# A two-layer hybrid decoder trunk: the RG-LRU ahead of the SSD's branch, and five smaller moves

## The chip, the cores and the metric

The kernel runs on one core of a Trainium2 chip. Its time is device microseconds (us) of one execution, the median of several runs. Times inside a profile count from the first instruction of the profiled execution.

## The reference, cut to what matters

256 tokens of width 1024 pass two layers, all in float32. `split` stands for the kernel's way of keeping precision: a matrix is taken apart into a high part (fp32r, the format TensorE multiplies in one pass) and the low rest, and a product is three matmuls.

```
c = silu(c);  shift1, scale1, gate1, shift2, scale2, gate2 = split6(c @ ada_w + ada_b)
h = rmsnorm(x) * n1 * (1 + scale1) + shift1
q, k, v, z, xbc, dt, lru_gate, lru_x, merge = split(h @ w_in)           # 16,416 columns
y_attn = three dilated window patterns, 24 heads, softmax over the patterns
y_ssd  = rmsnorm((ssd(silu(conv(xbc)), dt) + D*x) * silu(z), norm_g)    # 2048 wide, 8 groups
a = exp(-8 * sigmoid(x_r) * softplus(-lam))                             # RG-LRU, 1280 wide
y_lru  = scan(a, sqrt(1 - a*a) * sigmoid(x_i) * conv(lru_x)) * gelu(lru_gate)
x = x + gate1 * (sum_b sigmoid(merge_b) * (y_b @ w_br_b)) @ w_out
h = rmsnorm(x) * n2 * (1 + scale2) + shift2
# router: best of 4 groups, then the best 2 of its 8 experts, softmax weights
x = x + gate2 * sum_e weight_e * ((silu(h @ w_gate_e) * (h @ w_up_e)) @ w_down_e)   # 32 experts
out = rmsnorm(x) * final_g
```

## The kernel before

**Pages.** Nearly all data lies in one pool of 42 pages of 512 KB (`Pages`, L131). `Pages.live` counts the pages that are in use as the program is written down. Weights come as loads of one page each through the queue of SyncE (SP), in a fixed order (`Ring`, L148): `pump` writes down the next load while fewer than `ahead` loads stand ready and fewer than 42 - `reserve` pages are live; `take` hands the next one over, and writes its load down on the spot when none is ready. The pairs (ahead, reserve) of the stages stand at L23.

**Dense part.** A layer's products are jobs of 4 to 15 loads (`Job`, L1433). `go_on` (L629) walks the list of (job, load) steps. A step prepares the load four steps ahead (`LEAD`): ScalarE copies the high part `wh`, VectorE and GpSimd take turns at the low part `wl`; the SSD's branch weights are scaled by the norm's weight at the same time (L1449). Then it issues the matmuls of its own load (a step of a merge chunk or branch has 12 with 512 columns), finishes the job before if that is due, and lets at most three side threads run on to their next `yield` (`Side.tick`, L190); a `yield n` puts the thread off for n steps. Side threads are the attention pairs, SSD groups, z gates and the LRU. The planner that places instructions keeps, engine by engine, near to the order written. `act(...)` (L275) chains those ScalarE operations that need a function table.

The order of jobs in a layer is that of `_chunks` (L31): B, C, X and z twice (with the sums for the adaptive norms between), v, q and k; the SSD's merge chunks with its branch (16 loads); `lx`, `lxg`, `lg` for the LRU with the jobs of gate 1, the LRU's own gates (5 loads); the merge chunks and branches of attention and LRU; `w_out`. The LRU thread (`lru`, L1010) starts at the last gate product.

**Experts.** `out_half` (L1084) adds the two halves of the result to x and starts squares and logits. `moe` (L1203) makes the normalised x as `xnh`, has two jobs for the sums of gate 2 (`filler`), chooses experts (`route`), makes the low part `xnl`, and gathers the tokens of four experts as `xe` (`gather`). Then 16 steps of two experts follow: `up_part`, `combine` of the step before, `turn`, `down_part`. An expert has room for 64 tokens; a conditional block (`overflow`, L1361) recomputes the rest if any expert has more. It stands at step 15 and takes its pages from the pool.

Of the kernel before, what the change touches and what calls it, by code (L numbers as in the profile page):

```python
# [30 lines left out]
def _chunks():  # L31
# [20 lines left out]
    for n in range(2):  # L52
        put("m", (n, 1), MG0 + 1024 + 512 * n)
# [5 lines left out]
    for b in (0, 2):  # L59
        for n in range(2):  # L60
            put("m", (n, b), MG0 + 1024 * b + 512 * n)
# [157 lines left out]
class Trunk:  # L219
# [90 lines left out]
    def run(self):  # L310
# [26 lines left out]
        self.filler = {}  # L337
        jobs = self.jobs = [self.layer_jobs(l) for l in range(DEPTH)]
        loads = []
        for l in range(DEPTH):  # L340
            for phase in jobs[l]:
                loads += [j.loads[q] for j, q in phase if q is not None]
            for j in self.filler[l]:
                loads += j.loads
            loads += self.expert_loads(l)
# [60 lines left out]
    def ada_finish(self, job):  # L406
# [4 lines left out]
        if kind == "g":  # L411
            self.copy(co, job.banks[0])
            if i == 0:
                self.gate_page(l, 0)
            g = self.gate[l, i // 2]
            o = g[:, (i % 2) * 512:(i % 2) * 512 + 512]
            self.mm(p, bc(self.const("sel"), [128, 128]), co, True, i < 2)
            if i < 2:
                self.tt(o, p, o, OP.add)
            else:  # L420
                self.spread(p, o[0:1], False)
                self.copy(o, p)
# [101 lines left out]
    def logits(self, n):  # L524
# [3 lines left out]
        for kp in (2 * n, 2 * n + 1):  # L528
            p = self.x_T(kp, self.x)
            o = self.hT[kp // 2][:, 2 * (kp % 2):2 * (kp % 2) + 2]  # L530
# [8 lines left out]
    def layer_jobs(self, l):  # L539
# [89 lines left out]
    def go_on(self):  # L629
        pend = None  # L630
        for i, (j, q) in enumerate(self.seq):
# [5 lines left out]
            if j.kind == "out":  # L637
                self.ring.ahead, self.ring.reserve = OUT
                if q == 0:
                    self.gate_page(self.l, 1)  # L640
                    self.xnh = [self.pages.get([128, 1024], F32R, "xnh") for b in range(2)]
                    self.hT = [self.pages.get([128, 4, 256], F32, "hT") for b in range(2)]
# [73 lines left out]
    def chunk_done(self, job):  # L716
# [24 lines left out]
        elif kind in ("lx", "lxg", "lg"):  # L741
            for t in range(4):
# [7 lines left out]
                else:  # L750
# [3 lines left out]
                    self.copy(self.lg[ti // 4][:, ti % 4], src)  # L754
# [32 lines left out]
    def attn_pair(self, l, hp):  # L787
# [47 lines left out]
        yield 2  # L835
# [37 lines left out]
    def ssd_group(self, l, g):  # L873
# [49 lines left out]
        pz = self.ps().rearrange("p (j t) -> p j t", j=4)  # L923
        for j in range(2):
# [15 lines left out]
    def gate_z(self, l, i, z):  # L940
# [8 lines left out]
        self.split_act(hi, lo, y)  # L949
# [9 lines left out]
        if i == 3:  # L959
            self.yT[1] = self.zT  # L960
            yield 2
# [48 lines left out]
    def lru(self, l):  # L1010
# [3 lines left out]
        for u in range(3):  # L1014
# [3 lines left out]
            sq = self.third(u, "lsq")  # L1018
            self.act(sq, rp[u], AF.Square)
            self.stt(tp[u], sq, 1.0, tp[u], OP.add, OP.mult)  # L1020
            if u < 2:
                self.pages.free()
            yield 2
        for u in range(3):
            self.act(tp[u], tp[u], AF.Sqrt)
            self.tt(ip[u], ip[u], tp[u], OP.mult)
        yield 1
        for u in range(3):
            self.act(self.lg[u], self.lg[u], AF.Gelu_apprx_tanh)
        his, los = [], []  # L1030
        for u in range(3):
            hi, lo = self.third(u, "ylh", F32R), self.third(u, "yll", F32R)
            for t in range(sizes[u]):
                self.nc.vector.tensor_tensor_scan(tp[u][:, t], rp[u][:, t], ip[u][:, t], 0.0, OP.mult, OP.add)  # L1034
            self.tt(tp[u], tp[u], self.lg[u], OP.mult)
            self.split_act(hi, lo, tp[u])
# [4 lines left out]
            yield 2  # L1041
# [8 lines left out]
    def branch_done(self, job):  # L1050
# [14 lines left out]
        if n == 1:  # L1065
            self.pages.free(2 * min(len(self.yT[b][0]), 2 if b == 2 else 4))
# [136 lines left out]
    def moe(self, l):  # L1203
# [7 lines left out]
        for j in self.filler[l]:  # L1211
# [6 lines left out]
        pages.live -= 2  # L1218
        self.xnl = [pages.get([128, 1024], F32R, "xnl") for b in range(2)]
        for b in range(2):  # L1220
            self.stt(self.xnl[b], self.x[b], r[b], self.xnh[b].bitcast(F32), OP.mult, OP.subtract)
# [5 lines left out]
        def gather(j):  # L1227
# [6 lines left out]
            xe = [pages.get([128, 4, 256], F32, "xe") for h in range(2)]  # L1234
# [13 lines left out]
            Sf = S.bitcast(F32)  # L1248
# [14 lines left out]
            st[j] = (xe, ST, ws)  # L1263

        def up_part(i):
# [13 lines left out]
            if i % 2:  # L1279
                pages.free(2)  # L1280
# [50 lines left out]
        ye = None  # L1331
# [286 lines left out]
```

## Time and profile before

| | us |
|---|---|
| median of 3 runs (2285.91 to 2288.2) | 2286.91 |
| the profiled execution | 2287.82 |
| its span, first to last instruction | 2286.1 |
| PE busy in it | 2155.9 (94%) |
| VectorE (DVE) / ScalarE (ACT) / GpSimd (POOL) busy | 1125.2 / 802.5 / 440.8 |
| moved by DMA | 638.76 MB |

A busy PE is not PE at its peak: a matmul's record covers its way through the array, and they overlap. How many start in a stretch says more. Experts run in the stretches where DMA stands at 409 GB/s.

### The profile page before, as it was taken

The page shows a single profiled execution, that of the slowest core. Times are in us where ns is not written, and L with a number is a line of the kernel's source. Part 1 is how long each engine was busy: PE and PEld are TensorE (multiplying, and loading weights), DVE is VectorE, ACT ScalarE, POOL GpSimd, SP SyncE. Part 2 cuts the span into 40 slices and gives each one's busy share as a digit, 9 for nine tenths or more (in the row PEclk, how much of TensorE's full clock was granted, in tenths as well). Part 3 has the DMA queues.
Part 4 walks back from the last instruction along what each step waited for, and adds up shares of the span by engine and source line. Part 5 has one row for each costly group of instructions (what it writes and reads, how often), then busy time and mean ns, then how long its engine had stood idle before and what let it go on. Part 6 is the DMA issues. An engine that isn't in the chain of part 4 may idle for free.

```text
span 2286.1 us, 31957 instructions
## 1 busy us (share of the span) xinstructions
PE 2155.9 (94%) x12432; PEld 1428.4 (62%) x12432; DVE 1125.2 (49%) x1782; ACT 802.5 (35%) x1240; POOL 440.8 (19%) x189
## 2 busy tenths in 40 slices
PE   6999999999899999999989999999989999999997
PEld 4878798787674444333368988878868544443332
DVE  3877767653842222222258876774484322222222
ACT  3555644536531111101145655453474211111111
POOL 2333432232420000000023444212334000000000
PEclk9999999999999999999999999999999899999999
DMA  9565334574588999999994534447557799999996
GB/s 384 172 223 202 125 119 145 196 254 148 202 343 326 409 409 409 409 409 409 369 374 157 166 112 130 122 148 257 177 182 271 286 408 409 409 409 409 409 409 270
DMA packets 178524, 638.76 MB, mean 279 GB/s; under 512 B 20256, under 2 KB 20512, under 8 KB 178368
## 3 DMA queue, kind: packets, MB, share of 16 engines
q1 hardware_dynamic: 176976, 633.55, 74.2%
q8 instruction: 101, 1.65, 0.3%
q0 software_dynamic: 672, 1.74, 0.2%
q10 hardware_dynamic: 720, 1.37, 0.2%
q14 instruction: 55, 0.45, 0.1%
HBM read 635.53 MB, written 1.05 MB: 278 GB/s over the span
## 4 chain that ended last, share of the span: by engine, by line
PE 36%; DMA 7%; DVE 3%; ACT 2%; issue 2%; POOL 0%; DVEq 0%; SPq 0%; ACTq 0%; POOLq 0%
PE pm L265 29%; PE pside L265 6%; DMA w<-in_exp_u_dram 3%; DMA w<-in_exp_g_dram 3%; PE pside L273 1%; DMA w<-in_exp_d_dram 1%; ACT eaT L284 0%; DVE wl L1459 0%; ACT wh L284 0%; DVE Pb L296 0%; ACT Pb L281 0%; DVE lt L1034 0%; DVE mx L299 0%; ACT Pa L281 0%; DVE xbcX L287 0%
## 5 line engine op out<-in xcount | busy, mean ns | idle before, releaser
L1459 POOL TENSOR_TENSOR wl<-w,wh 128x1024 fp32r<-128x1024 f32 (+1 forms) x159 | 411.1, 2593 | 1234.2 <-ACT wh L284 669.9
L265 PE MATMUL pm<-w,xe 128*64 128x512 f32 x2048 | 502.8, 599 | 15.5 <-DMA w<-in_exp_u_dram 8.2
L265 PEld LDWEIGHTS pm<-w,xe 128*64 128x64 f32 x2048 | 166.3, 137 | 321.6 <-issue 238.3
L284 ACT ACTIVATE wh<-w 128x1024 fp32r<-128x1024 f32 (+1 forms) x316 | 306.2, 1012 | 44.0 <-DVE wl L1459 11.6
L265 PE MATMUL pm<-hh,wl 128*128 128x256 f32 x1056 | 303.0, 288 | 6.3 <-DVE wl L1459 4.4
L265 PE MATMUL pm<-hh,wh 128*128 128x256 f32 x1056 | 303.6, 288 | 4.9 <-ACT wh L284 3.1
L1459 DVE TENSOR_TENSOR wl<-w,wh 128x1024 fp32r<-128x1024 f32 (+1 forms) x157 | 267.0, 1704 | 68.3 <-ACT wh L284 65.0
L265 PE MATMUL pm<-hl,wh 128*128 128x256 f32 x1056 | 300.1, 284 | 0.0
L265 PE MATMUL pm<-w,eaT 128*64 128x512 f32 x1024 | 243.2, 597 | 22.2 <-ACT eaT L284 22.2
L287 DVE TENSOR_TENSOR ea<-ea,pm 128x512 f32<-128x512 f32 x32 | 22.0, 688 | 403.5 <-PE pm L265 403.5
L265 PEld LDWEIGHTS pm<-hh,wh 128*128 128x128 f32 x1056 | 203.4, 193 | 20.0 <-ACT wh L284 9.9
L265 PE MATMUL pm<-wh,hh 128*128 128x512 f32 (+1 forms) x544 | 205.6, 378 | 10.1 <-ACT sg L281 10.1
L265 PEld LDWEIGHTS pm<-hh,wl 128*128 128x128 f32 x1056 | 203.2, 193 | 11.5 <-DVE wl L1459 5.1
L265 PEld LDWEIGHTS pm<-hl,wh 128*128 128x128 f32 x1056 | 203.5, 193 | 1.0 <-issue 0.7
L265 PE MATMUL pm<-wh,hl 128*128 128x512 f32 (+1 forms) x544 | 201.8, 371 | 0.0
L265 PE MATMUL pm<-wl,hh 128*128 128x512 f32 (+1 forms) x544 | 201.8, 371 | 0.0
L265 PEld LDWEIGHTS pm<-w,eaT 128*64 128x64 f32 x1024 | 73.9, 137 | 159.4 <-issue 121.0
L281 ACT ACTIVATE ea<-pm 128x512 f32<-128x512 f32 x32 | 19.1, 597 | 298.2 <-PE pm L265 298.2
L265 PEld LDWEIGHTS pm<-wh,hh 128*128 128x128 f32 x544 | 104.1, 191 | 29.4 <-ACT sg L281 12.1
L284 ACT ACTIVATE eaT<-pside 128x512 f32<-128x512 f32 x32 | 19.1, 597 | 290.1 <-PE pside L273 290.1
L265 PEld LDWEIGHTS pm<-wl,hh 128*128 128x128 f32 x544 | 104.1, 191 | 12.8 <-issue 1.6
L265 PEld LDWEIGHTS pm<-wh,hl 128*128 128x128 f32 x544 | 103.7, 191 | 12.6 <-issue 0.7
(308 smaller groups left out, 2974.1 us busy)
## 6 DMA issues: line engine op xcount, KB each, us to landing
w<-in_exp_g_dram SPq DMA_DIRECT2D x256, 512.0 KB, 10.2
w<-in_exp_u_dram SPq DMA_DIRECT2D x256, 512.0 KB, 10.2
w<-in_exp_d_dram SPq DMA_DIRECT2D x256, 512.0 KB, 10.2
w<-in_w_in_dram SPq DMA_DIRECT2D x208, 512.0 KB, 4.1
w<-in_ada_w_dram SPq DMA_DIRECT2D x96, 512.0 KB, 5.0
w<-in_w_br_dram SPq DMA_DIRECT2D x60, 512.0 KB, 4.2
w<-in_w_in_dram SPq DMA_DIRECT2D x64, 384.0 KB, 3.1
w<-in_w_out_dram SPq DMA_DIRECT2D x16, 512.0 KB, 3.7
```

What stands on the lines that cost most here:

```text
L265: return self.nc.tensor.matmul(o, l, r, start=start, stop=stop, skip_group_check=True)
L273: self.nc.tensor.transpose(o, i, self.ident)
L281: self.table_op = self.nc.scalar.activation(out=o, in_=i, func=f, **kw).ins
L284: self.nc.scalar.activation(out=o, in_=i, func=AF.Copy)
L287: self.nc.vector.tensor_tensor(out=o, in0=x, in1=y, op=op)
L1459: eng.tensor_tensor(out=lo, in0=w, in1=hi.bitcast(F32), op=OP.subtract)
```

## The change

- The SSD's merge chunks and branch move behind the LRU's gate products. The LRU thread yields after nearly every operation or pair of scans.
- `gelu` is applied when the gate is copied from PSUM. The three parts of `lsq`, `ylh`, `yll` all use whole pages.
- The norm's weight is put on y (`hi`, `lo` by columns), no longer on the SSD's branch weights.
- The two jobs for gate 2 are ordinary jobs among the chunks of each layer; the bias of gate 2 is fetched broadcast, as that of gate 1.
- `xnl` is made right behind `xnh`, ahead of `route`; `xT` is no longer in `hT` pages.
- `ST` and `ws` of a group of experts are made after the first products (`ways_back`), `xe` and `ye` are held from the start.
- `overflow` stands at step 8 and counts its six pages; the reserves of the expert part change.
- In an SSD group the decay `E` is computed one stage later, in a bank that is in use anyway.

```diff
-N_PAGES, N_HALF = 42, 10
-DENSE, BRANCH, OUT, MOE, MOE_END = (4, 8), (99, 9), (99, 3), (99, 4), (99, 18)
+N_PAGES, N_HALF = 42, 11
+DENSE, BRANCH, OUT, MOE = (4, 8), (99, 9), (99, 4), (99, 0)
+IF_AT, MOE_IF, MOE_CLAIM, MOE_LAST = 8, 6, 7, 3
@@ _chunks
-    for n in range(2):
-        put("m", (n, 1), MG0 + 1024 + 512 * n)
     put("lx", 0, LX0)
...
-    for b in (0, 2):
+    for b in (1, 0, 2):
         for n in range(2):
             put("m", (n, b), MG0 + 1024 * b + 512 * n)
@@ gate_page
-        if i == 0:
-            self.nc.gpsimd.dma_start(g, bass.AP(tensor=src.tensor, offset=src.offset, ap=[[0, 128], [1, 1024]]))
-        else:
-            self.nc.gpsimd.dma_start(g[0:1], src)
+        self.nc.gpsimd.dma_start(g, bass.AP(tensor=src.tensor, offset=src.offset, ap=[[0, 128], [1, 1024]]))
@@ layer_jobs
+        extra += [self.ada_job(l, n, "g", i) for i, n in ((2, 10), (3, 11))]
-        self.filler[l] = [self.ada_job(l, n, "g", i) for i, n in ((2, 10), (3, 11))]
@@ chunk_done, "lg"
-                    self.copy(self.lg[ti // 4][:, ti % 4], src)
+                    self.act(self.lg[ti // 4][:, ti % 4], src, AF.Gelu_apprx_tanh)
@@ gate_z
-        self.split_act(hi, lo, y)
+        for t in range(4):
+            c = self.col(l, "sn")[:, 4 * i + t:4 * i + t + 1]
+            self.act(hi[:, t], y[:, t], AF.Copy, scale=c)
+            self.stt(lo[:, t], y[:, t], c, hi[:, t].bitcast(F32), OP.mult, OP.subtract)
@@ lru
         for u in range(3):
             self.act(tp[u], tp[u], AF.Sqrt)
+        yield 1
+        for u in range(3):
             self.tt(ip[u], ip[u], tp[u], OP.mult)
         yield 1
-        for u in range(3):
-            self.act(self.lg[u], self.lg[u], AF.Gelu_apprx_tanh)
...
-            hi, lo = self.third(u, "ylh", F32R), self.third(u, "yll", F32R)
             for t in range(sizes[u]):
                 self.nc.vector.tensor_tensor_scan(tp[u][:, t], rp[u][:, t], ip[u][:, t], 0.0, OP.mult, OP.add)
+                if t % 2:
+                    yield 1
             self.tt(tp[u], tp[u], self.lg[u], OP.mult)
-            self.split_act(hi, lo, tp[u])
+            yield 1
+            hi, lo = [self.pages.get([128, 4, 256], F32R, n)[:, 0:sizes[u]] for n in ("ylh", "yll")]
+            self.copy(hi, tp[u])
+            yield 1
+            self.tt(lo, tp[u], hi.bitcast(F32), OP.subtract)
...
-            yield 2
+            yield 1
@@ moe
             self.act(self.xnh[b], self.x[b], AF.Copy, True, scale=r[b])
+            self.stt(self.xnl[b], self.x[b], r[b], self.xnh[b].bitcast(F32), OP.mult, OP.subtract)
         self.warm(AF.Exp, r[1])
-        for j in self.filler[l]:
-            for q in range(4):
-                j.prepare(q)
-                j.product(q)
-            j.finish()
         rest = self.route(l, r)
...
+        xe = [pages.get([128, 4, 256], F32, "xe") for h in range(2)]
+        ye = [pages.get([128, 1024], F32R, n) for n in ("yeh", "yel")]
         gather(0)
...
         for i in range(16):
-            if i == 13:
-                ring.ahead, ring.reserve = MOE_END
-            if i == 15:
+            if i == IF_AT - 1:
+                ring.reserve = MOE_IF
+            if i == IF_AT:
                 self.table_op = None
                 self.overflow(l)
                 self.table_op = None
+                ring.reserve = MOE[1]
+            if i == 13:
+                ring.reserve = MOE_CLAIM
...
-            if i % 2 and i + 1 < 16:
+            if i % 2 == 0:
+                ways_back(i // 2)
+            elif i + 1 < 16:
                 gather(i // 2 + 1)
...
+            if i == 14:
+                ring.reserve = MOE_LAST
@@ Job.prepare
-        if self.kind == "branch" and self.arg[2] == 1:
-            s = T.col(self.arg[0], "sn")
-            for k in range(2):
-                c = s[:, 2 * q + k:2 * q + k + 1]
-                T.act(hi[:, k], w[:, k], AF.Copy, scale=c)
-                T.stt(lo[:, k], w[:, k], c, hi[:, k].bitcast(F32), OP.mult, OP.subtract)
-        else:
-            T.copy(hi, w)
...
+        T.copy(hi, w)
...
```

## Rows read from the trace of the kernel before

**Rows 1.** The page's slices: 40 equal parts of the span, DMA in GB/s.

```profile
GB/s 384 172 223 202 125 119 145 196 254 148 202 343 326 409 409 409 409 409 409 369 374 157 166 112 130 122 148 257 177 182 271 286 408 409 409 409 409 409 409 270
```

**Rows 2.** Windows, layer 1: length, busy (instructions) by engine, PEclk, DMA share, GB/s.

```profile
1650.00:1675.00 25.00, 25.00 (x126) 17.91 (x125) 12.52 (x13) 22.72 (x45) 6.95 (x4) 1.00 0.45 148
1675.00:1700.00 25.00, 20.89 (x83) 15.94 (x81) 24.96 (x26) 16.34 (x19) 8.07 (x3) 0.93 0.63 210
```

**Rows 3.** Timeline of PE: start, us, what, [idle before <-who ended it].

```profile
549.14 0.50 PE L265 MATMUL pm<-wh,hh 128*128 128x512 f32 x1
...
593.13 0.79 PE L265 MATMUL pm<-wh,hh 128*128 128x512 f32 x1 [4.32 <-ACT sg L281]
...
1660.72 0.50 PE L265 MATMUL pm<-wh,hh 128*128 128x512 f32 x1
...
1704.71 0.79 PE L265 MATMUL pm<-wh,hh 128*128 128x512 f32 x1 [5.05 <-ACT sg L281]
```

**Rows 4.** Chain of waits in order of time: start, us, what.

```profile
1704.71 29.57 PE pm L265 x120
...
1735.15 24.61 PE pm L265 x108
```

**Rows 5.** DVE groups, 1640 to 1712: count, busy us, mean ns, idle.

```profile
L1459 DVE TENSOR_TENSOR wl<-w,wh 128x1024 fp32r<-128x1024 f32 x9 | 12.4, 1374 | 3.1 <-ACT wh L284 3.1
...
L1034 DVE TENSOR_TENSOR_SCAN lt<-lr,li 128x256 f32<-128x256 f32 x10 | 6.1, 663 | 0.0
```

**Rows 6.** Timeline of PE, one gate job: its four loads, then its sum.

```profile
1590.70 1.92 PE L265 MATMUL pm<-w,c 128*32 128x512 f32 x16
...
1595.79 1.02 PE L265 MATMUL pside<-cond,cn 128*128 128x512 f32 x2
```

**Rows 7.** Waits on DVE: engine, line, <-whom: us in total, times, longest.

```profile
DVE gate L287 <- DMA gate<-in_ada_b_dram: 8.7, 2, 4.5
```

**Rows 8.** Timeline around the router: layer 0's low part first, then layer 1.

```profile
687.20 2.48 DVE L296 SCALAR_TENSOR_TENSOR xnl<-x,rs,xnh 128x1024 fp32r<-128x1024 f32 x2
...
1781.45 0.69 DVE L287 TENSOR_TENSOR ot<-pside,gate 128x512 f32<-128x512 f32 x1 [2.70 <-PE pside L265]
...
1788.89 0.35 DVE L296 SCALAR_TENSOR_TENSOR rgl<-pm,rs,rbias 128x4 f32<-128x4 f32 x2 [2.06 <-PE pm L265]
...
1793.68 0.23 DVE L287 TENSOR_TENSOR rA<-route,roh 128x64 fp32r<-128x64 f32 x1
...
1794.92 2.17 ACT L281 ACTIVATE xnh<-x,rs 128x1024 fp32r<-128x1024 f32 x2
...
1801.03 2.48 DVE L296 SCALAR_TENSOR_TENSOR xnl<-x,rs,xnh 128x1024 fp32r<-128x1024 f32 x2
...
1802.36 0.58 PE L265 MATMUL pside<-S,xnl 128*128 128x256 f32 x1 [2.65 <-DVE xnl L296]
...
1809.33 13.95 PE L265 MATMUL pm<-w,xe 128*64 128x512 f32 x64
```

**Rows 9.** Timeline of SP's expert loads: the last group of eight, and two after.

```profile
1782.60 5.17 SPq L170 DMA_DIRECT2D w<-in_exp_g_dram  x8
...
1799.46 0.33 SPq L170 DMA_DIRECT2D w<-in_exp_u_dram  x1
...
1811.27 0.80 SPq L170 DMA_DIRECT2D w<-in_exp_u_dram  x2
```

**Rows 10.** Windows around the conditional block (layer 0) and the gather (layer 1).

```profile
1120.00:1138.00 18.00, 15.18 (x68) 5.15 (x66) 2.79 (x4) 1.99 (x4) 0.00 (x0) 1.00 0.73 282
...
1800.00:1812.00 12.00, 9.64 (x62) 7.82 (x64) 6.24 (x14) 3.04 (x6) 0.00 (x0) 0.67 0.17 45
```

**Rows 11.** Instructions of tile wl, low parts: ns min/median/max, first and last start.

```profile
L1459 POOL TENSOR_TENSOR wl<-w,wh x159: 1833/2422/3409, 32.6 to 1767.1; 128x1024 fp32r<-128x1024 f32 x127, 128x768 fp32r<-128x768 f32 x32
L1459 DVE TENSOR_TENSOR wl<-w,wh x157: 940/1226/3427, 28.6 to 1764.2; 128x1024 fp32r<-128x1024 f32 x125, 128x768 fp32r<-128x768 f32 x32
```

**Rows 12.** The page's DMA issues: engine, count, size, us from issue to landing.

```profile
w<-in_w_br_dram SPq DMA_DIRECT2D x60, 512.0 KB, 4.2
```

More of the change, by code (lines that the diff above doesn't have):

```diff
@@ L529, in logits @@
             p = self.x_T(kp, self.x)
-            o = self.hT[kp // 2][:, 2 * (kp % 2):2 * (kp % 2) + 2]
+            o = self.half([128, 2, 256], "xT")
             self.copy(o[:, 0], p[:, 0])
@@ L639, in go_on @@
                 if q == 0:
-                    self.gate_page(self.l, 1)
-                    self.xnh = [self.pages.get([128, 1024], F32R, "xnh") for b in range(2)]
-                    self.hT = [self.pages.get([128, 4, 256], F32, "hT") for b in range(2)]
+                    self.xnh, self.xnl = [[self.pages.get([128, 1024], F32R, n) for b in range(2)] for n in ("xnh", "xnl")]
             self.prepare_to(i + (OUT_LEAD if j.kind == "out" else LEAD) + 1)
@@ L923, in ssd_group @@
         pz = self.ps().rearrange("p (j t) -> p j t", j=4)
+        for j in range(2):
+            for e in range(2):
+                h = 4 * g + 2 * j + e
+                self.mm(pz[64 * e:64 * e + 64, 2 + j], bc(self.av[:, 1, h:h + 1], [128, 64]), self.const("le"))
+        self.act(E, pz[:, 2:4], AF.Exp)
         for j in range(2):
@@ L960, in gate_z @@
             self.yT[1] = self.zT
-            yield 2
+            yield 5
             rz = self.k([128, 2], "rz", 2)
@@ L1065, in branch_done @@
         if n == 1:
-            self.pages.free(2 * min(len(self.yT[b][0]), 2 if b == 2 else 4))
+            self.pages.free(2 * len(self.yT[b][0]))
         if b == 2:
@@ L1209, in moe @@
             self.act(self.xnh[b], self.x[b], AF.Copy, True, scale=r[b])
+            self.stt(self.xnl[b], self.x[b], r[b], self.xnh[b].bitcast(F32), OP.mult, OP.subtract)
         self.warm(AF.Exp, r[1])
-        for j in self.filler[l]:
-            for q in range(4):
-                j.prepare(q)
-                j.product(q)
-            j.finish()
         rest = self.route(l, r)
[L1218 to L1221, printed above, removed]
         acol = self.acol[l]
@@ L1294, in down_part @@
         def down_part(i, aT, last=False):
-            yh = pages.get([128, 1024], F32R, "yeh")
-            yl = pages.get([128, 1024], F32R, "yel")
+            yh, yl = ye
             ws = st[i // 2][2][:, i % 2:i % 2 + 1]
@@ L1341, in moe @@
                 self.warm(AF.Sqrt, av[:, 0:1])
-            if ye is not None:
+            if i:
                 for n in range(2):
-                    combine(i - 1, ye, n)
+                    combine(i - 1, n)
             aT = turn(av)
-            if i % 2 and i + 1 < 16:
+            if i % 2 == 0:
+                ways_back(i // 2)
+            elif i + 1 < 16:
                 gather(i // 2 + 1)
@@ L1358, in moe @@
                 self.on_pool = False
-        pages.free(5)
+        pages.free(9)
     def overflow(self, l):
@@ L1366, in overflow @@
             hT = self.hT = [self.pages.get([128, 4, 256], F32, "hT") for h in range(2)]
+            ow = [self.pages.get([128, 2, 512], F32, "ow") for q in range(4)]
             for kp in range(4):
@@ L1380, in overflow @@
                     for q in range(4):
-                        t = self.pages.pool.tile([128, 2, 512], F32, name="ow", tag="page")
+                        t = ow[q]
                         nc.sync.dma_start(t, a[w][l, bass.ds(e, 1), q].rearrange("o p k n -> (o p) k n"))
@@ L1400, in overflow @@
                     for q in range(2):
-                        t = self.pages.pool.tile([128, 2, 512], F32, name="ow", tag="page")
+                        t = ow[2 * n + q]
                         nc.sync.dma_start(t, a["exp_d"][l, bass.ds(e, 1), 2 * n + q].rearrange("o p k n -> (o p) k n"))
@@ L1411, in overflow @@
                         self.stt(self.x[b][:, sl], t, self.wo[:, b, bass.ds(e, 1)], self.x[b][:, sl], OP.mult, OP.add)
-            self.pages.free(2)
+            self.pages.free(6)
     def final_gain(self):
```

51 lines of the change are left out of this document (16 added, 35 removed).

## The prediction

> **What bounds the kernel now.** I read the page's slices first, then tables of windows, the PE rows around its gaps, and SP's issues. The slices show two regimes, twice [rows 1]: in a layer's dense part DMA moves 112 to 286 GB/s in most slices; while the experts run it stands at 409, slice after slice. So the dense part is paid in PE time, the expert part in bytes. An expert load is 512 KB, at 409 GB/s 1.28 us, and there are 384 in a layer. The expert stretch thus ends a fixed time after its first products release pages: anything that makes those products start earlier moves the end by as much.
>
> The dense part has one large hole per layer. In layer 1 PE has 83 matmuls in 25 us, while DVE is busy 24.96 of 25 [rows 2]. The PE rows say where [rows 3]: from the first product of merge chunk (0, 0) to that of (0, 2) there are 144 matmuls, and 43.99 us pass, in both layers (549.14 to 593.13, 1660.72 to 1704.71). At the undisturbed pace of the chain of waits, 24.61 us for 108 matmuls or 0.228 each, they need 32.8 [rows 4]. The last wait is 5.05 us for ACT's sigmoid `sg`, and behind it the chain has 29.57 us for 120 matmuls that would need 27.3. In the code, `sg` stands behind the LRU's copies on ACT, and these wait for DVE's scans and products.
>
> **The change part by part.** *LRU ahead of the SSD's branch.* Behind the last gate product there are then 24 steps of merge and SSD branch, 24 x 12 x 0.228 = 65.7 us, and 36 before the first product that needs the LRU. Its thread takes 22 ticks, one per step. DVE's share in it is four operations over 2560 columns, 3.1 us each by the 1.23 of a 1024-column low part [rows 11], and ten scans at 0.66: 19 us; the low parts of 12 weights at 1.37 are another 16 [rows 5]. That is 35 of 65.7. The hole of 43.99 - 32.8 = 11.2, and 2.2 of the slow run behind it, goes: I take 13 us in each layer. Bounds: 6 (half stays) to 13.4. What is late next is the weights' preparation, below.
>
> *Norm weight on y, gelu at evacuation, E one stage later, `xT` in a half page.* Work moves, little is added. The SSD weights' two scaled copies and two subtractions become one of each, half of them on POOL; four column-wise steps per z chunk replace one. Gelu takes the place of a copy; each extra table change costs ACT 1.28 us beside a PE that is fed four steps ahead. I put nothing; without that cover, 0 to 2 us a layer.
>
> *Gate sums early.* Two jobs of four loads leave the router's stretch and go among the SSD's chunks. PE pays 1.92 for the loads' products and 1.02 for the sum over partitions [rows 6], twice: 5.9 us a layer. The bias page is now fetched whole, as gate 0's is, and DVE stood 8.7 us in two such waits [rows 7]; behind the waiting sum stand convolutions and low parts. PE's share of 4.35 is between 0 and all; nearest is the old wait, in which PE's chunk went on, so I take 1.5. Together 7.4 a layer. POOL's one issue a layer delays its next low part, which is needed four steps on.
>
> *Router.* In layer 1 the last half of x is begun at 1781.45; the logits reach DVE at 1788.89, the choice is done at 1793.91, but PE is then in the second gate job, and `xnl` runs only at 1801.03, since ACT made `xnh` at 1794.92, behind the jobs' copies [rows 8]. PE gathers from 1802.36, the first expert product starts at 1809.33. Without the jobs the logits come some 1.4 earlier (two stretches of 1.06 stood between them), at 1787.5; the choice costs DVE 5.0, the two `xnl` 2.5 beside it: 1795.0. Rank product, positions and S take some 1.6, partly beside `xnl`, so the gather starts near 1796.0. It took 5.96 for 28 of its 32 products, so 6.8, and 0.6 for the last evacuation: 1803.4, a gain of 6 (4 to 8). Layer 0 had the same with a gather that sped up: `xnl` at 687.20; I take 4 (2 to 6). The ways back move behind the first products, worth 1.2 of it.
>
> PE stands idle longer before this gather than now; its granted clock was 0.67 in 1800 to 1812 [rows 10], a mixture of 1.2 and 2.4 GHz, and I counted the gather at the lower pace. The Trainium skill (TensorE: Matmul & The Clock Gate, Part 1: The HAM clock gate) says that an idle array falls to half rate and must be busy again before it is let up. By that rule the whole gather runs low, as I have it; had I counted it at 2.4 GHz the gain would be 9 and the total 6 lower.
>
> *Pages.* At the first expert product 33 loads had been issued: four groups of eight, and one at 1799.46; the next came at 1811.27, when PE freed pages [rows 9]. Counted from the code, `xe` and `ye` are now held from the start: 42 - 11 = 31. The DMA queue is idle then, so two more loads are to be moved after it: 2.6 us a layer (0 to 2.6). The filler's eight loads no longer precede the experts, but the 31 land in time either way.
>
> *The If in the middle.* SP drains its loads there now, too: 282 GB/s over 18 us against 409 is a loss of 5.6 [rows 10]. In a stretch bound by bytes it costs the same at step 8. I put 0 (-5 to +3 a layer). Larger reserves and shares at the end change nothing while DMA stays at 409.
>
> Sum: -26 + 14.8 - 10 + 5.2 = -16. The profiled execution took 2287.82 (span 2286.1 and 1.7 around it), so 2271.8; the median of the runs is 0.9 lower: **2271**, its own range 2263 to 2279.
>
> **The rivals.** *The weights come late (slower).* In the SSD's branch 26 pages are now held (yz 8, LRU 8, the rest 10), four pairs are 8, and the pump stops at 34: twelve to sixteen loads a layer are issued only when they are taken, four steps = 10.9 us ahead of use, where eight steps were usual. Landing takes 4.2 [rows 12], ACT's copy 1.09 as half of `xnh` [rows 8], POOL's part 2.42, at most 3.41 [rows 11]: 7.7 to 8.7, so PE would not notice. But in each queue LRU work stands ahead; with 14 us on the way a step takes 14/4 = 3.5 instead of 2.73, and 32 loads cost 25: 2296. It decides from 12.7 us on, where 32 x 0.45 eats most of the 16. For it: ACT was busy 22.72 of 25 in the gates' stretch [rows 2]. Against: ACT and DVE have more room behind it.
>
> *The hole only shrinks.* DVE blocked by POOL, or ACT by a copy that waits, now inside the SSD's branch: half of 26 stays, 2284. DVE's low part took 1.23 at the median and up to 3.43 [rows 11], and POOL gets twelve more a layer. The Trainium skill (SBUF — State Buffer, Summary: rules for kernel authors) states that where DVE reads two inputs and GpSimd reads too, the second to issue waits out the first; the trace agrees, with 3.43 against 1.23. By it 12 x 2.2 = 26 us join DVE's 35, nearly what the stretch has; it would come out at this rival's time.
>
> *More is gained.* PE has small gaps of its own among the SSD's chunks; the sums vanish in them (-14.8 at most), or the pages' term doesn't show: 2257.
>
> *The If holds SP.* Before, SP waited for its own loads alone. If at step 8 it must wait for pages that PE frees, 25 loads ahead less 8 in flight is up to 17 x 1.15 = 20 us, say 15 a layer: 2301. Nothing in the trace shows such a wait.
>
> **How the numbers follow.** A measurement tells 0.2%, 4.6 us, from no change: faster is below 2282.3, slower above 2291.5. The forecast has 0.55, more gained 0.15, the shrunken hole 0.14 (0.05 of it below 2282.3), late weights 0.11, the held SP 0.05 (0.02 of these two within 0.2%). Faster 0.55 + 0.15 + 0.05 = 0.75, same 0.09 + 0.02 = 0.11, slower 0.14. The range runs from 2254, below the gain without the sums, to 2289, the hole's upper side and the bound of the DVE waits: it leaves out 0.04 below and 0.14 above.
>
> **What would show it.** Right: the windows of the merge and branch chunks all have some 110 matmuls in 25 us; no PE wait for `sg` over 1 us; from `ot` to the first expert product some 22 instead of 28 us in layer 1; 31 loads issued by then; 282 GB/s or so around step 8 and 409 up to the last load. Wrong: PE waits for `wh` or `wl` in the SSD's branch (late weights); DVE at 25 of 25 there (the hole moved); PE gaps in the SSD's chunks behind `gate`; a DMA gap over 10 us at the If.

## The result: 38 us slower, and where they are in the profile after

The changed kernel takes 2325.62 us (median of 4 runs, 2325.17 to 2327.94) against 2287.33 beside it: a ratio of 1.017, 95% interval 1.0152 to 1.0188. The prediction was 2271, with 2254 to 2289 as its range. The profiled execution took 2325.38, its span 2323.6.

Five marks in either trace end the five stages of a layer: DVE's first `rot` (q and k chunks begin), ACT's last `kT`, DVE's first `ot` (the result of `w_out`), PE's first expert product, and DVE's last `x<-x,pside`.

| stage, us in layer 0 / layer 1 | before | after | difference |
|---|---|---|---|
| start to the first q/k chunk | 298.8 / 247.1 | 316.1 / 263.6 | +17.3 / +16.5 |
| q/k chunks | 98.3 / 98.7 | 97.6 / 98.1 | -0.7 / -0.6 |
| last q/k chunk to `w_out` (LRU, branches) | 263.7 / 264.3 | 271.9 / 271.8 | +8.2 / +7.5 |
| router and gather | 33.7 / 36.4 | 28.0 / 28.0 | -5.7 / -8.4 |
| experts | 468.4 / 468.5 | 468.4 / 471.2 | 0.0 / +2.7 |

They sum to 36.8 of the 37.5 us between the spans. Two stages lost, and of these the LRU's was forecast as the main gain.

The page's slices have the same two regimes as before [rows 1]; the expert slices stay at 409:

```profile
GB/s 382 172 209 209 159 138 148 171 111 174 262 326 290 409 409 409 378 409 409 409 360 176 181 135 124 114 138 185 124 256 237 282 409 409 409 378 410 409 409 284
```

The hole moved with the LRU. Windows of layer 1 (columns as in [rows 2]), now beside the SSD's branch:

```profile
1632.00:1657.00 25.00, 24.01 (x111) 16.57 (x111) 12.07 (x12) 23.45 (x44) 8.61 (x4) 1.00 0.34 108
1657.00:1682.00 25.00, 18.38 (x69) 14.35 (x68) 24.59 (x19) 14.64 (x16) 12.20 (x5) 0.87 0.48 166
1682.00:1707.00 25.00, 25.00 (x110) 20.64 (x110) 14.32 (x14) 13.71 (x15) 10.73 (x4) 0.99 0.54 189
```

PE runs 69 matmuls where the windows beside have 110, and DVE is busy for 24.59 of 25. PE's timeline names the wait, which answers to the 5.05 us of [rows 3]:

```profile
1676.51 0.80 PE L265 MATMUL pm<-wl,yzh 128*128 128x512 f32 x1 [5.65 <-DVE wl L1442]
1677.10 0.63 PE L265 MATMUL pm<-wh,yzl 128*128 128x512 f32 x1
1677.53 0.63 PE L265 MATMUL pm<-wh,yzh 128*128 128x512 f32 x1
```

The wait is for a low part of DVE, and matmuls behind it start 0.43 us apart instead of 0.228 [rows 4]: the hole is paid a second time at the low clock. DVE's timeline, and under it GpSimd's, show what the low part stood behind:

```profile
1661.73 1.23 DVE L287 TENSOR_TENSOR li<-li,lt 128x1024 f32<-128x1024 f32 x1 [0.37 <-ACT lt L281]
1662.99 3.94 DVE L1022 TENSOR_TENSOR_SCAN lt<-lr,li 128x256 f32<-128x256 f32 x3
1666.86 6.17 DVE L287 TENSOR_TENSOR li<-li,lt 128x1024 f32<-128x1024 f32 x2
...
1675.25 1.21 DVE L1442 TENSOR_TENSOR wl<-w,wh 128x1024 fp32r<-128x1024 f32 x1
```

```profile
1662.72 2.50 POOL L1442 TENSOR_TENSOR wl<-w,wh 128x1024 fp32r<-128x1024 f32 x1 [4.19 <-ACT wh L284]
1666.77 2.41 POOL L1442 TENSOR_TENSOR wl<-w,wh 128x1024 fp32r<-128x1024 f32 x1 [1.54 <-ACT wh L284]
1669.46 3.01 POOL L1442 TENSOR_TENSOR wl<-w,wh 128x1024 fp32r<-128x1024 f32 x1 [0.29 <-ACT wh L284]
```

A DVE operation with both inputs in SBUF that starts here while GpSimd makes a low part ends only half a us to 1.1 us behind GpSimd's end: the first of the three scans ran from 1662.99 to 1665.77, GpSimd's subtraction from 1662.72 to 1665.22. So two `li` products took 6.17 us, and the three scans 3.94 (0.66 each undisturbed [rows 5]).

In the first stage PE stops behind the second gate job. PE, then DVE, then ACT:

```profile
1316.42 0.39 PE L265 MATMUL pm<-hh,wl 128*128 128x256 f32 x1 [3.96 <-DVE wl L1442]
```

```profile
1309.14 0.69 DVE L287 TENSOR_TENSOR gate<-pside,gate 128x512 f32<-128x512 f32 x1 [1.09 <-PE pside L265]
1309.75 3.32 DVE L296 SCALAR_TENSOR_TENSOR yzl<-xbcX,cols,yzh 128x256 fp32r<-128x256 f32 x4
1313.00 6.70 DVE L1442 TENSOR_TENSOR wl<-w,wh 128x1024 fp32r<-128x1024 f32 x2
```

```profile
1308.07 1.06 ACT L278 ACTIVATE z<-xbcX 128x1024 f32<-128x1024 f32 x1 [3.10 <-DVE cb L881]
1309.03 1.69 ACT L278 ACTIVATE yzh<-xbcX,cols 128x256 fp32r<-128x256 f32 x4
1310.63 6.72 ACT L284 ACTIVATE wh<-w 128x1024 fp32r<-128x1024 f32 x7
```

ACT waits for DVE, the gate sum and the four column-wise copies and subtractions of a z chunk come first, and then seven high parts are due at once. GpSimd's rows of the same time show that DVE is held here, too:

```profile
1309.27 2.73 POOL L944 TENSOR_TENSOR zsum<-zsum,z 128x512 f32<-128x512 f32 x2 [4.98 <-ACT z L278]
1312.70 5.92 POOL L1442 TENSOR_TENSOR wl<-w,wh 128x1024 fp32r<-128x1024 f32 x2 [0.70 <-DVE yzl L296]
```

Of the four subtractions the first two took 1.10 and 1.51 us, beside `zsum`, and the last two 0.47 each; the low part that PE waits for ran from 1313.00 to 1316.37 beside GpSimd's from 1312.70 to 1315.28.

The router, which answers to [rows 8]:

```profile
1824.01 0.69 DVE L287 TENSOR_TENSOR ot<-pside,gate 128x512 f32<-128x512 f32 x1 [2.64 <-PE pside L265]
...
1834.36 0.22 DVE L287 TENSOR_TENSOR rA<-route,roh 128x64 fp32r<-128x64 f32 x1
...
1836.54 2.47 DVE L296 SCALAR_TENSOR_TENSOR xnl<-x,rs,xnh 128x1024 fp32r<-128x1024 f32 x2
```

```profile
1836.37 1.19 PE L265 MATMUL pside<-S,xnh 128*128 128x256 f32 x4 [0.71 <-DVE S L287]
...
1843.54 0.65 PE L265 MATMUL pm<-w,xe 128*64 128x512 f32 x2
```

From `ot` of the last half to the first expert product 19.5 us pass instead of 27.9; `xnl` still runs behind the choice. The windows around the conditional block (layer 0, then 1) answer to [rows 10]:

```profile
940.00:960.00 20.00, 17.43 (x74) 6.56 (x71) 1.92 (x4) 1.23 (x2) 0.00 (x0) 0.91 0.81 314
...
2075.00:2095.00 20.00, 20.00 (x103) 9.01 (x101) 3.75 (x7) 1.19 (x2) 0.00 (x0) 0.92 0.82 322
```

At 409 GB/s as the rate, 314 over 20 us is a loss of 4.6 us and 322 one of 4.3, about 1 us less than the 5.6 counted at step 15.

### The profile page after: what moved, and what is told of

It is laid out like the page before. It is cut to its first block, busy times and chain, and to the rows that moved or that the text cites. A ratio compares the mean times of both kernels' runs of the same rounds, so it can differ in the third digit from the quotient of the medians.

```text
span 2323.6 us, 31904 instructions
## 1 busy us (share of the span) xinstructions
PE 2177.8 (94%) x12424; PEld 1434.8 (62%) x12424; DVE 1128.3 (49%) x1762; ACT 804.3 (35%) x1226; POOL 475.8 (20%) x205
## 3 DMA queue, kind: packets, MB, share of 16 engines
q0 software_dynamic: 896, 2.78, 0.4%
## 5 line engine op out<-in xcount | busy, mean ns | idle before, releaser
L1442 POOL TENSOR_TENSOR wl<-w,wh 128x1024 fp32r<-128x1024 f32 (+1 forms) x175 | 450.7, 2582 | 1246.0 <-ACT wh L284 1125.0
L265 PE MATMUL pm<-w,xe 128*64 128x512 f32 x2048 | 494.5, 600 | 7.6 <-DVEq L1354 5.2
L284 ACT ACTIVATE wh<-w 128x1024 fp32r<-128x1024 f32 (+1 forms) x348 | 342.0, 1017 | 103.1 <-PE pm L265 32.0
L1442 DVE TENSOR_TENSOR wl<-w,wh 128x1024 fp32r<-128x1024 f32 (+1 forms) x173 | 296.2, 1720 | 128.4 <-ACT wh L284 120.9
L265 PEld LDWEIGHTS pm<-w,xe 128*64 128x64 f32 x2048 | 158.8, 137 | 306.9 <-issue 266.5
L265 PE MATMUL pm<-hh,wh 128*128 128x256 f32 x1056 | 309.3, 293 | 5.8 <-ACT wh L284 4.1
L265 PE MATMUL pm<-wh,hh 128*128 128x512 f32 (+1 forms) x544 | 199.6, 371 | 0.0
L284 ACT ACTIVATE yeh<-yt 128x512 fp32r<-128x512 f32 x64 | 40.3, 630 | 248.1 <-DVE yt L296 247.2
L287 DVE TENSOR_TENSOR x<-x,pside 128x512 f32<-128x512 f32 x128 | 83.4, 683 | 81.4 <-PE pside L265 80.5
L296 DVE SCALAR_TENSOR_TENSOR yt<-pm,ws,gate 128x512 f32<-128x512 f32 x64 | 48.1, 751 | 147.1 <-PE pm L265 147.1
## 6 DMA issues: line engine op xcount, KB each, us to landing
w<-in_exp_g_dram SPq DMA_DIRECT2D x256, 512.0 KB, 10.2
w<-in_exp_u_dram SPq DMA_DIRECT2D x256, 512.0 KB, 10.2
w<-in_exp_d_dram SPq DMA_DIRECT2D x256, 512.0 KB, 10.2
```

The lines of the kernel that those rows point to most:

```text
L265: return self.nc.tensor.matmul(o, l, r, start=start, stop=stop, skip_group_check=True)
L284: self.nc.scalar.activation(out=o, in_=i, func=AF.Copy)
L287: self.nc.vector.tensor_tensor(out=o, in0=x, in1=y, op=op)
L296: self.nc.vector.scalar_tensor_tensor(out=o, in0=x, scalar=s, in1=y, op0=op0, op1=op1)
L1442: eng.tensor_tensor(out=lo, in0=w, in1=hi.bitcast(F32), op=OP.subtract)
```

## The experiments

All medians and ratios to the kernel before, which ran beside each (2286.07 to 2288.56); stages as above, layer 0 / 1.

| run | median | ratio (95%) | start to q/k | to `w_out` | router | experts |
|---|---|---|---|---|---|---|
| e1 gates back | 2315.46 | 1.0123 (1.0106-1.0140) | 305.2 / 256.2 | 270.4 / 270.4 | 32.9 / 33.2 | 469.3 / 471.8 |
| e2 SSD first | 2311.96 | 1.0107 (1.0091-1.0124) | 315.2 / 263.4 | 266.3 / 266.3 | 28.0 / 27.0 | 467.9 / 471.4 |
| e3 both back | 2305.41 | 1.0084 (1.0067-1.0101) | 302.8 / 256.4 | 266.0 / 266.5 | 33.6 / 33.5 | 469.4 / 470.9 |
| e4 DVE alone | 2312.89 | 1.0109 (1.0093-1.0126) | 317.1 / 263.1 | 267.5 / 266.7 | 26.7 / 26.6 | 468.5 / 470.4 |
| e5 norm on weights | 2309.72 | 1.0099 (1.0082-1.0116) | 308.4 / 255.3 | 271.6 / 271.9 | 28.0 / 28.0 | 468.7 / 471.0 |
| e6 E as before | 2331.14 | 1.0189 (1.0172-1.0206) | 315.8 / 266.5 | 271.3 / 270.2 | 28.0 / 28.0 | 468.5 / 473.5 |
| e7 reserve 4 | 2313.91 | 1.0110 (1.0094-1.0127) | 317.1 / 263.1 | 266.6 / 269.0 | 27.1 / 27.1 | 469.0 / 471.7 |
| e8 bias early | 2331.36 | 1.0192 (1.0175-1.0209) | 316.9 / 267.2 | 273.3 / 272.7 | 28.0 / 26.8 | 468.3 / 471.4 |
| e9 both back, norm | 2292.51 | 1.0027 (1.0017-1.0036) | 297.4 / 253.3 | 265.6 / 265.0 | 32.3 / 33.6 | 468.3 / 472.4 |
| e10 LRU relieved | 2291.07 | 1.0015 (1.0005-1.0026) | 307.7 / 255.2 | 263.0 / 263.1 | 26.6 / 26.7 | 468.8 / 470.1 |
| e11 e10, gates back | 2284.55 | 0.9995 (0.9985-1.0004) | 297.4 / 250.5 | 260.7 / 261.9 | 32.8 / 33.4 | 468.4 / 471.4 |
| e12 e9, DVE alone | 2284.82 | 0.9998 (0.9988-1.0007) | 295.8 / 253.4 | 261.7 / 261.7 | 33.3 / 33.7 | 469.1 / 471.5 |
| e13 LRU's part alone | 2308.74 | 1.0107 (1.0090-1.0124) | 299.4 / 247.5 | 272.5 / 272.6 | 35.9 / 36.0 | 467.9 / 467.9 |
| e14 e13 relieved | 2289.14 | 1.0016 (1.0007-1.0025) | 299.5 / 246.3 | 262.7 / 262.4 | 37.2 / 37.0 | 468.4 / 469.3 |
| e15 early low part | 2288.18 | 1.0014 (1.0005-1.0023) | 300.8 / 246.9 | 264.0 / 264.1 | 33.1 / 35.6 | 469.9 / 470.2 |
| e16 e14 and e15 | 2285.14 | 0.9997 (0.9988-1.0006) | 299.1 / 247.2 | 263.6 / 262.8 | 32.5 / 33.6 | 468.8 / 470.2 |
| e17 before, DVE alone | 2280.88 | 0.9965 (0.9951-0.9979) | 298.3 / 245.7 | 262.3 / 262.6 | 34.2 / 34.4 | 467.8 / 468.8 |

**e1, e2, e3: the two large parts undone, each alone and together.** e1:

```diff
-        extra += [self.ada_job(l, n, "g", i) for i, n in ((2, 10), (3, 11))]
+        self.filler[l] = [self.ada_job(l, n, "g", i) for i, n in ((2, 10), (3, 11))]
...
+                    self.gate_page(self.l, 1)
```

> The changed kernel, with the two jobs for the sums of gate 2 back in the router's stretch (the bias page fetched ahead of them, as before). Theory A: the jobs cost the changed kernel 15 to 17 us a layer among the SSD's chunks (PE's own 5.9, and stalls of the SSD groups, gates and low parts that the short steps push together), so the stretch from the layer's start to the last q/k chunk gets 30 to 33 us shorter over both layers, and the router's stretch gets back some 6 to 8 us a layer: 2325.6 - 32 + 14 = about 2308. Rival B: the jobs cost PE's 5.9 alone, and the rest of the 16 comes from the norm's weight on y and from the later E: 2325.6 - 12 + 14 = about 2328.

10.2 us faster, between the two; the gate sums are put back as before, with the bias page fetched at the first load of `w_out`. The jobs cost 10.9 / 7.4 in the first stage and 1.5 / 1.4 behind it, 21.2 in all, and the router had won 4.9 / 5.2 by their going. e2:

```diff
+    for n in range(2):
+        put("m", (n, 1), MG0 + 1024 + 512 * n)
     put("lx", 0, LX0)
...
-    for b in (1, 0, 2):
+    for b in (0, 2):
```

> The changed kernel, with the SSD's merge chunks and branch back ahead of the LRU's chunks; the finer steps of the LRU and all else stay. Theory A: the new place of the LRU costs some 8 us a layer against the old one, since its work meets GpSimd's low parts and late loads: about 2325.6 - 16 = 2310. Rival B: the place gains, as predicted, up to 13 us a layer, and the loss comes from what the LRU does in finer steps and from gelu's table loads: this kernel is then slower than the changed one, 2335 to 2350. Rival C: both places have the same hole: 2326.

Theory A: 13.7 us faster, 5.6 / 5.5 of it in the LRU's stage. e3 has both edits.

> The changed kernel with both of these undone: gate sums in the router's stretch, the SSD's branch ahead of the LRU. What is left is the norm's weight on y, gelu at evacuation, the later E, finer steps, the low part of x ahead of the choice, pages and the conditional block at step 8. Theory A: the two parts carry the whole loss and add up: 2286 to 2294, about the kernel before. Rival B: the small edits carry 10 us or more a layer: over 2305.

Rival B: 17 us stay, 4.0 / 9.3 of them in the first stage. The small edits were not small.

**e4 and e7: why the LRU's stage is slow.** e4:

```diff
-        eng = T.nc.gpsimd if T.nsplit % 2 == 0 or T.on_pool else T.nc.vector
+        alone = (self.kind == "branch" and self.arg[2] == 1
+                 or self.kind == "tok" and self.arg[1] == "m" and self.arg[2][1] == 1)
+        eng = T.nc.gpsimd if (T.nsplit % 2 == 0 or T.on_pool) and not alone else T.nc.vector
```

> The changed kernel, with all low parts of the SSD's merge chunks and branch on VectorE, none on GpSimd, which leaves VectorE undisturbed while the LRU runs. Theory A: in the hole VectorE is held by GpSimd (operations of 1.2 us took 2.6 to 3.4); without it the LRU and the low parts take 19 + 24 x 1.22 = 48 us of the 66 that the steps have, and the wait of 5.6 us and its shorter ones go: 8 to 9 us a layer, about 2309. Rival B: the loads come late (no load is issued ahead of its use there), so the waits stay: 2322 to 2326. Rival C: VectorE has too much to do, and twelve more low parts make the hole deeper: 2335.

12.7 us faster, 4.4 / 5.1 of it in the LRU's stage, though DVE has twelve low parts more per layer. Its timeline shows the same operations as in the changed kernel, now with nothing of GpSimd's beside them:

```profile
1656.51 1.22 DVE L287 TENSOR_TENSOR li<-li,lt 128x1024 f32<-128x1024 f32 x1 [2.53 <-ACT lt L281]
1657.65 1.22 DVE L1443 TENSOR_TENSOR wl<-w,wh 128x1024 fp32r<-128x1024 f32 x1
1658.79 1.82 DVE L287 TENSOR_TENSOR li<-li,lt 128x1024 f32<-128x1024 f32 x2
1660.53 3.01 DVE L1022 TENSOR_TENSOR_SCAN lt<-lr,li 128x256 f32<-128x256 f32 x5
```

1.82 for the pair that took 6.17; five scans in 3.01. That is the rule of the Trainium skill (SBUF — State Buffer, Summary: rules for kernel authors) cited in the prediction, and the traces agree: the second one to issue waits out the first, as the scan at 1662.99 above. e7:

```diff
+            if q == 0 and j.kind == "lru":
+                self.ring.ahead, self.ring.reserve = 4, 4
```

> The changed kernel, with the ring's reserve at 4 pages instead of 8 from the LRU's gate products to the switch for the branches, so that none of the fifteen loads a layer that waited for their use does so any more. Theory A (GpSimd holds VectorE): the waits on low parts stay, 2322 to 2326. Rival B (the loads come late): the waits in the SSD's branch go, and 5 to 10 us a layer with them, 2306 to 2316.

Rival B's time: 11.7 us faster, 5.3 / 2.8 of it in this stage. In the changed kernel fifteen loads a layer are issued only when they are taken, and ACT stood for them; its waits (engine, for whom: us, times, longest) there:

```profile
ACT wh L284 <- DMA w<-in_w_br_dram: 23.3, 16, 3.6
```

No such row is left in e7. PE's waits from 500 to 660 us (layer 0), the changed kernel first, then e4, then e7:

```profile
PE pm L265 <- DVE wl L1442: 7.1, 3, 5.6
```

```profile
PE pm L265 <- DVE wl L1443: 3.6, 3, 2.7
```

```profile
PE pm L265 <- DVE mg L296: 1.9, 1, 1.9
PE pm L265 <- DVE wl L1444: 1.9, 1, 1.9
```

e4 leaves loads late (ACT's row for them is still 13.1, 10, 3.3), and e7 leaves GpSimd beside DVE. So either relief takes about half of the wait: a low part that starts late and a DVE that is held add up, and PE has only four steps in hand. e10 took both.

**e5, e6, e8: the first stage.** e5 puts `split_act(hi, lo, y)` back in `gate_z` and the scaled copies back in `prepare`:

```diff
+        if self.kind == "branch" and self.arg[2] == 1:
+            s = T.col(self.arg[0], "sn")
+            for k in range(2):
+                c = s[:, 2 * q + k:2 * q + k + 1]
+                T.act(hi[:, k], w[:, k], AF.Copy, scale=c)
+                T.stt(lo[:, k], w[:, k], c, hi[:, k].bitcast(F32), OP.mult, OP.subtract)
```

> The changed kernel, with the norm's weight back on the SSD's branch weights (y is split in one copy and one subtraction). With both large parts undone 17 us were still lost against the kernel before, 4 us of layer 0 and 9 of layer 1 between the layer's start and the first q/k chunk, where the z gates finish. Theory A: these come from the four column-wise copies and subtractions of each z chunk, which stand ahead of the low parts on VectorE: the stretch up to the first q/k chunk gets 4 to 9 us a layer shorter, the SSD's branch pays at most 4 us a layer for its scaled weights: about 2325.6 - 13 + 4 = 2316. Rival B: they come from the later E and the longer pauses of side threads: no change but in the branch, 2326 to 2332.

Theory A: 15.9 us faster, 7.7 / 8.3 in the first stage, and nothing lost in the branch. The wait of 3.96 us at the same place is 1.50, and the subtraction before it one of 1.54 us instead of 3.32:

```profile
1305.11 0.39 PE L265 MATMUL pm<-hh,wl 128*128 128x256 f32 x1 [1.50 <-DVE wl L1446]
```

```profile
1301.28 1.54 DVE L287 TENSOR_TENSOR yzl<-xbcX,yzh 128x1024 fp32r<-128x1024 f32 x1 [0.28 <-ACT yzh L284]
```

DVE's time for all of them, in the changed kernel and then in e5:

```profile
L296 DVE SCALAR_TENSOR_TENSOR yzl<-xbcX,cols,yzh 128x256 fp32r<-128x256 f32 x32 | 27.0, 901 | 8.2 <-ACT yzh L278 8.2
L287 DVE TENSOR_TENSOR yzl<-xbcX,yzh 128x1024 fp32r<-128x1024 f32 x8 | 12.0, 1497 | 12.3 <-ACT yzh L284 12.3
```

That is 15.0 us more. It is not the number of steps alone: in each group of four the first one or two took 1.09 to 1.52 us, each beside a `zsum` sum on GpSimd, and the others 0.47 (but for one beside a low part of GpSimd's, 2.06). No run moves `zsum`, so how much of the 16 us it makes is not shown.

e5 also qualifies e4. It takes the branch's eight low parts off GpSimd, and yet the LRU's stage gains nothing (271.6 / 271.9): DVE makes them in two column-wise steps each. Windows of layer 0, the changed kernel, e5 and e4:

```profile
530.00:555.00 25.00, 19.38 (x73) 15.43 (x73) 24.57 (x21) 12.56 (x13) 11.26 (x4) 0.86 0.48 163
530.00:555.00 25.00, 17.76 (x65) 12.94 (x64) 24.96 (x30) 11.02 (x15) 5.46 (x2) 0.86 0.39 137
530.00:555.00 25.00, 21.94 (x90) 17.45 (x89) 22.44 (x26) 15.91 (x17) 0.00 (x0) 0.93 0.62 217
```

Of the three, PE has most matmuls where DVE is least full, whether GpSimd's hold or its own steps fill it.

e6 makes `E` where the kernel before makes it, and has its pauses (2 steps in place of 3 in an attention pair, 2 in place of 5 ahead of the z statistics):

```diff
-            yield 5
+            yield 2
```

> The changed kernel, with the decay E of an SSD group made one stage earlier in a bank of its own, and with the shorter pauses of the attention pair (2 for 3) and of the z statistics (2 for 5), all as before. Theory A of the run before this (the norm's weight on y): no change here, 2324 to 2327. Rival B (the later E holds each group's last products until ScalarE has made it): the stretch up to the first q/k chunk gets 4 to 9 us a layer shorter, about 2313.

5.5 us slower, outside both expectations: the later `E` and the longer pauses together were a gain. e8:

```diff
+            if self.kind == "ada" and q == 0 and self.arg[2] == "g" and self.arg[3] % 2 == 0:
+                T.gate_page(self.arg[0], self.arg[3] // 2)
```

> The changed kernel, with each gate's bias page asked for when its first load is prepared, some eight steps before the sum that reads it. VectorE then no longer stands 2.3 to 7.2 us for it. Theory A: that wait starts a chain (VectorE, then ScalarE, then the low parts, then PE) in each of the two places: 3 to 5 us a layer, about 2317. Rival B: PE has work enough through the wait: within 2 us of 2325.6.

A miss for both: 5.7 us slower. DVE's wait for the bias page went from 16.2 us to nothing, but its waits for the same sum's product on PE came to 28.5 in place of 2.9: the wait was not what cost. Why it is slower is not settled.

**e9 to e12: the parts put together.** e9 is e3 with e5's edit.

> The changed kernel with three parts undone: gate sums in the router's stretch, the SSD's branch ahead of the LRU, the norm's weight on the branch weights. If the parts add up (theory A), this is 2305.4 - 16 = about 2289, the time of the kernel before, with gelu at evacuation, finer steps, the later E, the low part of x ahead of the choice and the new pages left in it. Rival B: the norm's weight on y cost so much only where gate jobs stand beside it: 2297 or more.

12.9 us under e3 and 6.4 over the kernel before, between the two theories; layer 1's first stage keeps 6.2 us, which no run here explains. e10 is the changed kernel with e5's and e7's edits, and e4's for the merge chunks (the branch's low parts are DVE's by e5).

> The changed kernel, with the order kept (LRU ahead of the SSD's branch, gate sums early), the norm's weight on the branch weights, whose low parts VectorE then makes alone, the low parts of the SSD's merge chunks on VectorE too, and a reserve of 4 from the LRU's gate products on. Theory A (VectorE held by GpSimd, and late loads, are two causes of the same stretch, each worth some 5 us a layer, and the order itself gains once both are gone): from the last q/k chunk to w_out 258 to 262 us a layer instead of 272, and with the 16 us of the norm's weight 2285 to 2291. Rival B: both relieve one and the same wait, so the stretch stays at 266 as with either alone: 2298.

The time is at theory A's end, the stage between the two: 263, 9 us under the changed kernel's and only 1 under that of the kernel before. e11 adds e1's edit.

> The run before this one in the list, and the gate sums back in the router's stretch. If the gate jobs cost what they did (10 us net), 10 us faster than that one: 2275 to 2281 by theory A, 2288 by rival B. If they cost less where VectorE has room (rival C), within 4 us of it.

6.5 us less than e10, between the 10 and the 4 that were expected; no difference from the kernel before can be told. e12 is e9 with e4's line for attention's chunks and branch (`arg[2] == 0`, `arg[2][1] == 0`), where the LRU runs at its old place.

> The first kernel of this list (three parts undone), with the low parts of attention's merge chunks and branch on VectorE alone, which is where the LRU runs at its old place. Theory A: the hole there too was VectorE held by GpSimd (5.7 us of stretched operations) and goes in part: 3 to 6 us a layer, about 2280. Rival B: the hole is the LRU's chain itself (35 us of work in 33 us of steps), and twelve more low parts deepen it: 2289 to 2297.

Theory A in the stage: 3.9 / 3.3 us less than e9's, and at 261.7 as good as at the new place in e11 (260.7 / 261.9). The time is 7.7 us under e9, though 5 above that theory's.

**e13 to e16: parts of the change alone, on the kernel before.** e13 has the new order of `_chunks`, the new `lru`, and gelu at evacuation.

> The kernel before, with the LRU's part of the change alone: the SSD's merge chunks and branch behind its gate products, finer steps, gelu at evacuation, whole pages. Theory A (late loads, and VectorE held by GpSimd where low parts of merge chunks go to it, cost more than the hole gave): as in the changed kernel, from the last q/k chunk to w_out 270 to 272 us a layer instead of 264, and 2286.5 + 15 = about 2301. Rival B (the place gains, and only norm and gate jobs spoiled it): 258 to 262 a layer, 2278.

Theory A, and more: 22.7 us slower. The stage loses 8.8 / 8.3 by the new place, the finer steps and gelu together; putting the place alone back in e2 gave 5.6 / 5.5. e14 adds the two reliefs at once, so it does not show what each is worth here:

```diff
+                self.ring.ahead, self.ring.reserve = 4, 4
...
+            alone = self.kind == "tok" and self.arg[1] == "m" and self.arg[2][1] == 1
```

> The run before this one in the list, with a reserve of 4 pages from the LRU's gate products on, and VectorE alone making the low parts of the SSD's merge chunks. Theory A: the stretch comes to 261 us a layer, 3 less than in the kernel before, so 2286.5 - 6 = about 2281. Rival B: the relief gives back only what the place cost: within 2 us of the kernel before.

The stage gains 1.0 / 1.9 against before, but the router loses 3.5 / 0.6: neither theory's time. PE's waits from 500 to 660 us, e13 and then e14:

```profile
PE pm L263 <- DVE wl L294: 6.3, 3, 3.0
```

```profile
PE pm L263 <- DVE mg L294: 1.4, 1, 1.4
```

Of the 9.8 us between them in layer 0, idle PE is 4.9 (11.3 and 6.4 over the stage) and 5.0 the granted clock (6.8 and 1.8, windows of some 10 us, one minus the clock each). In this count, which takes idle time at the low clock twice, a hole is paid about twice. e15:

```diff
             self.act(self.xnh[b], self.x[b], AF.Copy, True, scale=r[b])
+            self.stt(self.xnl[b], self.x[b], r[b], self.xnh[b].bitcast(F32), OP.mult, OP.subtract)
```

> The kernel before, with the low part of x made right behind its high part, ahead of the jobs of gate 2 and the choice, and the transposed x in half pages; the jobs stay in the router's stretch. Theory A: PE's wait of 2.65 us for it in the gather goes, the rest stands: some 2.5 us a layer, 2281. Rival B: its 2.5 us on VectorE now stand ahead of the choice, and the gather starts so much later: within 1 us of the kernel before.

Nothing gained: 2.1 us slower, somewhat beyond rival B's 1 us. e16 joins e14 and e15.

> The two runs before this one in the list joined: LRU ahead of the SSD's branch with both reliefs, and the low part of x made early. If both gain by theory A they add up: 2286.5 - 6 - 5 = about 2276. If one of them falls, the other's time.

As the kernel before: 3 to 4 us under either part, but the gains of theory A did not come.

**e17: the cause used on the kernel before.**

```diff
-            eng = T.nc.gpsimd if T.nsplit % 2 == 0 or T.on_pool else T.nc.vector
+            alone = (self.kind == "branch" and self.arg[2] == 0
+                     or self.kind == "tok" and self.arg[1] == "m" and self.arg[2][1] == 0)
+            eng = T.nc.gpsimd if (T.nsplit % 2 == 0 or T.on_pool) and not alone else T.nc.vector
```

> The kernel before, with one edit that is not part of the change: the low parts of attention's merge chunks and branch, beside which the LRU runs there, are all made by VectorE, none by GpSimd. Theory A (about half of the 11 us of the hole is VectorE held by GpSimd): from the last q/k chunk to w_out 261 to 262 us a layer instead of 264, as in e12, so 2286 - 5 = about 2281. Rival B: what the stretch gives is lost at the router and the experts, as it was in e14: within 2 us of the kernel before.

2280.88, ratio 0.9965 (0.9951 to 0.9979): faster than both kernels, at theory A's time. But the LRU's stage gains 1.4 / 1.7, less than theory A had; the rest is spread over the stages. DVE in layer 0, before first, then e17:

```profile
581.87 3.34 DVE L287 TENSOR_TENSOR yll<-lt,ylh 128x1024 fp32r<-128x1024 f32 x1
```

```profile
579.84 1.20 DVE L287 TENSOR_TENSOR yll<-lt,ylh 128x1024 fp32r<-128x1024 f32 x1
```


## Why the prediction was wrong, step by step

- **LRU ahead of the SSD's branch (-13 a layer): wrong, the largest error.** The step "the hole of 11.2 goes" priced DVE's 35 us of 65.7 at undisturbed durations. Measured: +8.2 / +7.5, alone +8.8 / +8.3. DVE was full there instead (24.59 of 25 us in 1657 to 1682), and PE waited 5.65 us for its low part. The two slower rivals named the right mechanisms and were priced as if only one came, and from a hole already gone. DVE held by GpSimd: without it e4 is 12.7 us faster. Late weights: without them e7 is 11.7 us faster. The count of 12 to 16 loads was right (15); the 7.7 to 8.7 us counted to prepare one of the 10.9 left some 2 for a queue on DVE. With both gone the stage is 1 to 3 us a layer shorter than before (e14, e11), not 13, and the old place does as well once GpSimd is off it (e12, e17). So the place as such is not shown to gain anything.
- **Norm's weight on y (0): wrong, 16 us.** "Work moves, little is added" looked at the branch's weights, where nothing was won (e5). The cost is where the z gates finish: DVE already was busy 23.66 and 22.10 of 25 there before (layer 1, 1238 to 1288), and the steps that came to it took 15.0 us more in all, most of it beside GpSimd's `zsum`.
- **Gate sums early (+14.8): too small, 21.2 by e1,** 18.5 between e10 and e11. Beyond the 11.8 us that were counted for PE itself, which no run measured apart, the jobs cost some 9 in place of 3. That is not the wait for the bias page, which that term was for: e8 takes it away and is slower. Which stalls make it up is open.
- **Router (-10): right in kind, -14.1.** The jobs' going gave 4.9 / 5.2 (e1). `xnl` was not made beside the choice, as the step had it, but behind it; PE's wait for it was 0.31 us nevertheless, and alone the step won nothing (e15). The gather did run at the lower pace at which it was counted: in layer 1 its products start some 0.21 us apart up to 1842.7, and 0.12 from 1843.0 on.
- **Pages (+5.2): half.** 33 loads were issued by the first product, not 31; layer 0 lost nothing, layer 1 2.7.
- **The If (0): not contradicted.** By the windows above the block costs about 1 us less than before; no run moved it alone.
- **Gelu, later E, `xT` (0 together):** the later E, put at nothing, and the longer pauses, which no term named, together gained 5.5 (e6); gelu was not tried by itself.

By these terms: LRU +16 for -26, norm +16 for 0, gates +21 for +15, router -14 for -10, pages +3 for +5, E and pauses -5.5 for 0, which is 36 where 38 was measured. The sum proves little: the LRU's term and the gates' share 2.9 us of one stage, and the parts do not add up in e9 either.

## What to carry to other kernels

Price VectorE's two-input work at its blocked duration wherever GpSimd works beside it, and where VectorE is as full as here (22 to 25 of 25 us), expect operations put ahead of a PE input to cost PE time. In three kernels of this case GpSimd's share of such a stretch was better done by VectorE itself (e4, e12, e17); in e5, where VectorE needed two steps for each, it was not. Before work is moved to a roomier stretch, count the pages it holds there: a prefetch that shrinks to nothing and a held engine meet in the same wait.

## What the runs showed of the hardware

A scan of 128x256 takes 0.66 us alone and was 2.78 beside a GpSimd subtraction (three of them 3.94); a product of 1.2 us came to 3.4, and a column-wise subtraction of 0.47 to 1.1 to 1.5 beside a GpSimd sum. An idle stretch of 5.65 us was followed by matmuls 0.43 us apart, where 0.228 was the undisturbed pace; the granted clock over the window of 25 us was 0.87, a mixture of 1.2 and 2.4 GHz.
